# The sum of an attention accumulator's two halves and the gating move from VectorE to GpSimd, with a second ScalarE copy

## The chip, the core and the metric

The kernel runs on one core of a Trainium2 chip. The metric is the device time of one execution in microseconds (us), as the median of several runs; smaller is better.

## What is computed

The reference is a two-layer decoder trunk over 1024 positions of width 1024, all in float32. Each layer normalises its input and projects it; two attention mixers read the projections. The change touches only the end of each mixer: its output is multiplied by its own gate.

```python
# stick-breaking attention, 8 heads of 64
w = where(strict, exp(log_sigmoid(z) + between), 0)      # between: reversed cumulative sum of log_keep
a = einsum('bhqk,bhkd->bqhd', w, v)
a = a.reshape(B, S, SB_WIDTH) * silu(sb_z)
# native sparse attention, 8 heads in 2 groups: compressed, selected and window branches
b = g[0] * o_cmp + g[1] * o_slc + g[2] * o_win
b = b * silu(n_z)
y = sigmoid(m_a) * (a @ w_proj_a) + sigmoid(m_b) * (b @ w_proj_b)
x = x + gate * (y @ w_out)
```

## The kernel before

A layer runs in stages. First come the projections that both mixers need. Then the sparse attention (method `nsa`) and the stick-breaking attention (method `sb`) run one after the other, and in both of them the remaining projections are strewn in on TensorE as filler, by a planner with a fixed cost for each piece. The rest of the filler and the output projections end the layer. In the profiled execution the sparse stage lies from about 316 to 684 us in the first layer and from 1340 to 1735 in the second, the stick-breaking stage from 684 to 945 and from 1735 to 2005.

Every matrix product keeps float32 accuracy by splitting one operand into a high part and a low part, each in the faster float32r format. ScalarE writes the high part (line 136) and VectorE the difference (line 137). The values V lie in memory as 64 columns of high parts beside 64 columns of low parts, so a value product leaves an accumulator `av` of 128 partitions in PSUM: 64 partitions for the high half, 64 for the low half of one head, times 256 query positions. The two halves still have to be added. PSUM holds one such accumulator (`bufs=1`).

The methods that the change touches do this:

- `merge` (line 929 on, stick-breaking stage): ScalarE copies one half to the SBUF tile `mt` (line 935, with a shift of 64 partitions), and VectorE adds the other half to it, reading PSUM, and writes 64 partitions of the output tile `o` (line 936). Two heads share one tile of 128 partitions.
- `finish_pair` (line 921 on): after the odd head of a pair SyncE loads the gate `szl` (line 925), VectorE multiplies (line 926) and SyncE stores to the array AD in HBM (line 927).
- `nsa_merge` (line 1191 on) and `nsa_finish` (line 1199 on) are the same for the sparse stage, with a tile of 64 partitions by 512 columns (two heads side by side), lines 1195, 1196, 1205 to 1207.

One job of the stick-breaking stage is one head and one block m of 256 queries, m = 0 to 3, thus 32 jobs in a layer; a job has two rows of tiles, x = 0 and 1, with 128(2m + x + 1) keys. For each row TensorE computes the scores (lines 885, 886, 888), ScalarE two sigmoids C and E (lines 1298, 1299), VectorE a reversed running product over C (the scan, line 1302) and the product of E with it (line 1303). TensorE transposes E (line 898), ScalarE and VectorE split it into `wh` and `wl` (lines 136, 137), and TensorE multiplies it with the values (lines 917, 918). GpSimd sets one column of C to 1 (line 1294). The scores of a job and the value products of the job before are traced in turn, and `merge` is the last step of the latter.

Each engine works through its queue in order. Who waits for whom is set by semaphores from the data dependencies; the order within a queue is laid out by a scheduler at build time. SyncE's queue holds most DMAs, GpSimd's holds the loads of AD and of a few gates for the output stage (lines 1392, 1458). The tiles `mt` and `szl` have one buffer each.

Of the kernel before, what the change touches and what calls it, by code (L numbers as in the profile page):

```python
# [15 lines left out]
ALU = mybir.AluOpType  # L16
# [71 lines left out]
class Trunk:  # L88
# [832 lines left out]
    def finish_pair(self, pool, o, row, m, gate_row):  # L921

        nc = self.nc
        sz = self.tl(pool, [P, 256], F32, "szl", bufs=1)
        nc.sync.dma_start(sz, self.SZ[gate_row:gate_row + P, m * 256:m * 256 + 256])
        nc.vector.tensor_tensor(o, o, sz, ALU.mult)
        nc.sync.dma_start(self.AD[row:row + P, m * 256:m * 256 + 256], o)

    def merge(self, pool, ps, o, par):

        nc = self.nc
        a = par * 64
        b = 64 - a
        t = self.tl(pool, [P, 256], F32, "mt", bufs=1)
        nc.scalar.copy(t[a:a + 64], ps[b:b + 64, 0:256])
        nc.vector.tensor_tensor(o[a:a + 64], ps[a:a + 64, 0:256], t[a:a + 64], ALU.add)


    def nsa_load_kv(self, g):
# [251 lines left out]
    def nsa_merge(self, pool, ps, o):  # L1191

        nc = self.nc
        t = self.tl(pool, [64, 256], F32, "mt", bufs=1)
        nc.scalar.copy(t, ps[64:128, 0:256])
        nc.vector.tensor_tensor(o, ps[0:64, 0:256].rearrange("p (h t) -> p h t", h=2),
                                t.rearrange("p (h t) -> p h t", h=2), ALU.add)

    def nsa_finish(self, pool, o, hd, m):

        nc = self.nc
        sz = self.tl(pool, [64, 2, 256], F32, "szl", bufs=1)
        c = slice(m * 256, m * 256 + 256)
        r = hd * 64
        nc.sync.dma_start(sz, self.SZ[r:r + P, c].rearrange("(h d) t -> d h t", d=64))
        nc.vector.tensor_tensor(o, o, sz, ALU.mult)
        nc.sync.dma_start(self.AD[512 + r:512 + r + P, c].rearrange("(h d) t -> d h t", d=64), o)

    def av_stages(self, pool, m, es, v):
# [302 lines left out]
```

## Time and profile before

| | |
|---|---|
| median of 3 runs | 2184.01 us (2183.47 to 2190.08) |
| the profiled execution, whole | 2188.37 us |
| its span, which the rows below count | 2186.6 us |
| TensorE busy | 2096.8 us, 96% |
| VectorE busy | 1575.6 us, 72% |
| ScalarE busy | 1130.8 us, 52% |
| GpSimd busy | 72.4 us, 3% |
| DMA | 136 GB/s on average |

The engines are named PE (TensorE), PEld (its weight loads), DVE (VectorE), ACT (ScalarE), POOL (GpSimd) and SP (SyncE) in the profile; a trailing q is an engine's instruction queue. A row names the line of the kernel, the engine, the operation and the tiles, output before input. The ends of matmuls are modelled, and they overlap, so a busy TensorE isn't TensorE at its peak. Who released a wait is inferred from semaphores.

### The profile page before, as it was taken

How to read it: one execution, taken by the hardware profiler on the slowest of the kernel's cores; microseconds unless marked ns; L12 is line 12 of the kernel's file. 1: busy time of each engine (PE TensorE's matmuls, PEld its weight loads, DVE VectorE, ACT ScalarE, POOL GpSimd, SP SyncE). 2: the span in 40 equal slices, each digit the busy share in tenths (PEclk: the TensorE clock that was granted, in tenths of full speed). 3: DMA queues.
4: the chain of work that ended last, by engine and by line, in shares of the span. 5: the costliest groups of instructions: out<-in, count | busy, mean ns of one | idle time of the engine just before them, and what ended most of it. 6: DMA issues, size and time to landing. Idle time of an engine off the chain costs nothing.

```text
span 2186.6 us, 36378 instructions
## 1 busy us (share of the span) xinstructions
PE 2096.8 (96%) x12952; PEld 1817.6 (83%) x12952; DVE 1575.6 (72%) x3698; ACT 1130.8 (52%) x2465; POOL 72.4 (3%) x242
## 2 busy tenths in 40 slices
PE   3999999999999999999999999999999999999999
PEld 3899788988988777779799987889898877777899
DVE  5758568878867778786866763887788687778643
ACT  4433137666666656563533422765666656556410
POOL 2200000000000000010001000000000000001000
PEclk8999999999999999999999999999999999999999
DMA  7445933244226454175456465222532444534433
GB/s 292 96 150 169 287 121 103 87 124 126 80 64 149 126 140 125 64 252 180 157 170 167 137 180 150 84 90 86 145 97 83 121 127 113 145 100 167 154 123 104
DMA packets 254102, 297.02 MB, mean 136 GB/s; under 512 B 38888, under 2 KB 201568, under 8 KB 253920
## 3 DMA queue, kind: packets, MB, share of 16 engines
q1 hardware_dynamic: 213152, 250.65, 38.3%
q10 hardware_dynamic: 36224, 29.37, 5.3%
q0 software_dynamic: 4544, 14.68, 2.4%
q8 instruction: 102, 1.67, 0.3%
q14 instruction: 80, 0.66, 0.1%
HBM read 206.28 MB, written 83.89 MB: 133 GB/s over the span
## 4 chain that ended last, share of the span: by engine, by line
PE 72%; DVE 15%; DMA 4%; issue 4%; ACT 3%; POOL 1%; SPq 0%; DVEq 0%; ACTq 0%; POOLq 0%
PE proj L194 16%; PE proj L198 16%; PE proj L196 16%; PE tr L898 6%; DVE C L1302 5%; PE av L918 4%; PE av L917 3%; PE sc L885 3%; PE sc L886 3%; DVE E L1303 3%; DVE wl L137 2%; DVE w L137 1%; ACT wh L136 1%; DMA ada<-in_ada_w 1%; DMA actlo<-AD 1%
## 5 line engine op out<-in xcount | busy, mean ns | idle before, releaser
L194 PE MATMUL proj<-acthi,w 128*128 128x512 f32 x1312 | 537.5, 410 | 3.4 <-DVE sz L833 2.1
L198 PE MATMUL proj<-acthi,w 128*128 128x512 f32 x1312 | 536.9, 409 | 0.8 <-DVE w L137 0.8
L196 PE MATMUL proj<-actlo,w 128*128 128x512 f32 x1312 | 534.5, 407 | 0.5 <-DVE actlo L137 0.5
L136 ACT CAST w<-raw 128x512 fp32r<-128x512 f32 (+1 forms) x296 | 183.5, 623 | 219.4 <-PE proj L198 111.3
L137 DVE TENSOR_TENSOR wl<-tr,wh 128x512 fp32r<-128x512 f32 (+2 forms) x408 | 255.8, 639 | 46.1 <-ACT wh L136 44.4
L194 PEld LDWEIGHTS proj<-acthi,w 128*128 128x128 f32 x1312 | 249.8, 190 | 40.6 <-DVE sz L833 2.5
L196 PEld LDWEIGHTS proj<-actlo,w 128*128 128x128 f32 x1312 | 249.3, 190 | 37.7 <-DVE actlo L137 1.9
L198 PEld LDWEIGHTS proj<-acthi,w 128*128 128x128 f32 x1312 | 249.0, 190 | 37.5 <-DVE w L137 1.3
L136 ACT CAST wh<-tr 128x512 fp32r<-128x512 f32 (+2 forms) x408 | 219.2, 550 | 87.7 <-PE tr L898 84.7
L137 DVE TENSOR_TENSOR w<-raw,w 128x512 fp32r<-128x512 f32 (+1 forms) x296 | 203.3, 690 | 85.0 <-ACT w L136 83.6
L194 PE MATMUL proj<-w,acthi 128*128 128x256 f32 (+1 forms) x768 | 222.0, 289 | 7.1 <-ACT G L813 3.3
L198 PE MATMUL proj<-w,actlo 128*128 128x256 f32 (+1 forms) x768 | 221.3, 288 | 0.0
L196 PE MATMUL proj<-w,acthi 128*128 128x256 f32 (+1 forms) x768 | 220.5, 287 | 0.0
L898 PE MATMUL tr<-ident,E 128*128 128x128 f32 x1152 | 188.7, 275 | 26.1 <-DVE E L1303 25.5
L918 PE MATMUL av<-wl,V 128*128 128x256 f32 (+1 forms) x776 | 202.1, 287 | 5.5 <-DVE wl L137 5.5
L917 PE MATMUL av<-wh,V 128*128 128x256 f32 (+1 forms) x776 | 202.0, 278 | 0.4 <-ACT E L1146 0.2
L898 PEld LDWEIGHTS tr<-ident,E 128*128 128x128 f32 x1152 | 140.3, 140 | 72.0 <-DVE E L1303 40.6
L1302 DVE TENSOR_TENSOR_SCAN C<-C 128x128 f32<-128x128 f32 (+7 forms) x128 | 173.1, 1352 | 34.3 <-ACT C L1298 33.6
L885 PE MATMUL sc<-kk,q 128*128 128x512 f32 (+3 forms) x512 | 174.2, 340 | 2.1 <-DVE mx L1143 0.9
L886 PE MATMUL sc<-kk,q 128*128 128x512 f32 (+3 forms) x512 | 174.5, 341 | 0.0
L918 PEld LDWEIGHTS av<-wl,V 128*128 128x128 f32 x776 | 146.0, 188 | 25.7 <-DVE wl L137 13.0
L917 PEld LDWEIGHTS av<-wh,V 128*128 128x128 f32 x776 | 146.4, 189 | 13.7 <-ACT wh L136 3.2
(250 smaller groups left out, 3911.1 us busy)
## 6 DMA issues: line engine op xcount, KB each, us to landing
raw<-in_w_in SPq DMA_DIRECT2D x168, 256.0 KB, 3.3
ada<-in_ada_w SPq DMA_DIRECT2D x48, 512.0 KB, 5.5
kk<-QK SPq DMA_DIRECT2D x48, 512.0 KB, 7.7
q<-QK ACTq DMA_DIRECT2D x64, 256.0 KB, 4.6
QK<-s SPq DMA_DIRECT2D x32, 512.0 KB, 3.1
MD<-sz SPq DMA_DIRECT2D x64, 256.0 KB, 2.6
QK<-s SPq DMA_DIRECT2D x48, 256.0 KB, 4.2
VD<-s SPq DMA_DIRECT2D x48, 256.0 KB, 2.1
```

Of the source, the lines that this page charges most:

```text
L136: nc.scalar.copy(hi, src)
L137: nc.vector.tensor_tensor(lo, src, hi.bitcast(F32), ALU.subtract)
L194: nc.tensor.matmul(ps, lh, rh, start=(x == 0), stop=False)
L196: nc.tensor.matmul(ps, lh, rl, start=False, stop=False)
L198: nc.tensor.matmul(ps, ll, rh, start=False, stop=(x == n - 1))
L885: nc.tensor.matmul(ps, q, k[:, 0, c0:c1], start=True, stop=False)
L886: nc.tensor.matmul(ps, q, k[:, 1, c0:c1], start=False, stop=not masks)
L898: nc.tensor.transpose(pt[:, x * P:x * P + P], b, self.ident)
L917: nc.tensor.matmul(ps[:, c:d], lhsT, hi[:, a:b], start=(first and x == 0), stop=False, skip_group_check=True)
L918: nc.tensor.matmul(ps[:, c:d], lhsT, lo[:, a:b], start=False, stop=(last and x == n - 1), skip_group_check=True)
L1302: nc.vector.tensor_tensor_scan(rev, rev, rev, 1.0, ALU.mult, ALU.bypass)
L1303: nc.vector.tensor_tensor(e[:, 0:nk], e[:, 0:nk], c[:, 1:nk + 1], ALU.mult)
```

## The change

In both attention stages ScalarE copies both halves of the accumulator to SBUF, the first to `mt` as before, the second to the output tile `o`. GpSimd adds `mt` to `o` in place, and GpSimd, not VectorE, multiplies the finished tile by the gate. The loads and stores around them stay on SyncE's queue.

```diff
@@ finish_pair
         nc.sync.dma_start(sz, self.SZ[gate_row:gate_row + P, m * 256:m * 256 + 256])
-        nc.vector.tensor_tensor(o, o, sz, ALU.mult)
+        nc.gpsimd.tensor_tensor(o, o, sz, ALU.mult)
         nc.sync.dma_start(self.AD[row:row + P, m * 256:m * 256 + 256], o)
@@ merge
         nc.scalar.copy(t[a:a + 64], ps[b:b + 64, 0:256])
-        nc.vector.tensor_tensor(o[a:a + 64], ps[a:a + 64, 0:256], t[a:a + 64], ALU.add)
+        nc.scalar.copy(o[a:a + 64], ps[a:a + 64, 0:256])
+        nc.gpsimd.tensor_tensor(o[a:a + 64], o[a:a + 64], t[a:a + 64], ALU.add)
@@ nsa_merge
         nc.scalar.copy(t, ps[64:128, 0:256])
-        nc.vector.tensor_tensor(o, ps[0:64, 0:256].rearrange("p (h t) -> p h t", h=2),
-                                t.rearrange("p (h t) -> p h t", h=2), ALU.add)
+        nc.scalar.copy(o, ps[0:64, 0:256].rearrange("p (h t) -> p h t", h=2))
+        nc.gpsimd.tensor_tensor(o, o, t.rearrange("p (h t) -> p h t", h=2), ALU.add)
@@ nsa_finish
         nc.sync.dma_start(sz, self.SZ[r:r + P, c].rearrange("(h d) t -> d h t", d=64))
-        nc.vector.tensor_tensor(o, o, sz, ALU.mult)
+        nc.gpsimd.tensor_tensor(o, o, sz, ALU.mult)
```

## Rows read from the trace of the kernel before

**Rows 1.** Busy time by stage: stretch, its length, PE, PEld, DVE, ACT, POOL.

```profile
316.00:684.00 368.00, 365.78 (x2371) 322.28 (x2370) 290.28 (x880) 238.46 (x563) 1.94 (x13) 1.00 0.36 105
684.00:945.00 261.00, 245.18 (x1404) 198.80 (x1403) 209.69 (x280) 162.09 (x355) 11.60 (x68) 1.00 0.44 122
1340.00:1735.00 395.00, 392.98 (x2494) 343.52 (x2493) 301.60 (x927) 245.92 (x583) 1.41 (x10) 1.00 0.35 102
1735.00:2005.00 270.00, 254.17 (x1449) 205.87 (x1448) 215.06 (x290) 165.31 (x362) 11.77 (x70) 1.00 0.44 121
```

**Rows 2.** Waits of TensorE: us in total, times, longest.

```profile
PE tr L898 <- DVE E L1303: 25.5, 38, 1.1
...
PE av L918 <- DVE wl L137: 5.5, 12, 0.9
```

**Rows 3.** Timeline of VectorE, one head of stick-breaking: start, us, instruction.

```profile
789.57 1.75 DVE L1302 TENSOR_TENSOR_SCAN C<-C 128x768 f32<-128x768 f32 x1
791.45 0.96 DVE L1303 TENSOR_TENSOR E<-E,C 128x768 f32<-128x768 f32 x1
...
799.14 2.28 DVE L1302 TENSOR_TENSOR_SCAN C<-C 128x1024 f32<-128x1024 f32 x1
801.56 1.23 DVE L1303 TENSOR_TENSOR E<-E,C 128x1024 f32<-128x1024 f32 x1
```

**Rows 4.** Timeline of TensorE, the same head, with idle time before.

```profile
792.47 0.55 PE L898 MATMUL tr<-ident,E 128*128 128x128 f32 x3 [0.50 <-DVE E L1303]
...
802.84 0.55 PE L898 MATMUL tr<-ident,E 128*128 128x128 f32 x3 [0.33 <-DVE E L1303]
```

**Rows 5.** Groups by line, VectorE: busy us, mean ns, idle before.

```profile
L936 DVE TENSOR_TENSOR o<-av,mt 64x256 f32<-64x256 f32 x64 | 26.7, 417 | 31.6 <-ACT mt L935 30.8
L1196 DVE TENSOR_TENSOR o<-av,mt 64x256 f32<-64x256 f32 x64 | 26.5, 414 | 27.9 <-ACT mt L1195 27.5
...
L1206 DVE TENSOR_TENSOR o<-o,szl 64x512 f32<-64x512 f32 x32 | 21.8, 682 | 0.3
...
L926 DVE TENSOR_TENSOR o<-o,szl 128x256 f32<-128x256 f32 x32 | 13.5, 423 | 0.8
```

**Rows 6.** The chain that ended last: start, us on it, what.

```profile
323.89 0.04 DVE o L1196
...
850.11 0.38 ACT mt L935
...
857.99 0.44 DVE o L936
...
1995.51 0.33 DVE o L926
```

**Rows 7.** Timeline of ScalarE, the same head, with idle time before.

```profile
784.40 0.60 ACT L1298 ACTIVATE C<-sc 128x512 f32<-128x512 f32 x1 [0.21 <-PE sc L886]
...
789.99 0.37 ACT L935 COPY mt<-av 64x256 f32<-64x256 f32 x1 [0.28 <-PE av L918]
791.48 0.60 ACT L1298 ACTIVATE C<-sc 128x512 f32<-128x512 f32 x1 [1.13 <-PE sc L886]
...
799.98 0.37 ACT L935 COPY mt<-av 64x256 f32<-64x256 f32 x1 [0.73 <-PE av L918]
...
801.96 0.28 ACT L1298 ACTIVATE C<-sc 128x128 f32<-128x128 f32 x1 [1.62 <-PE sc L888]
```

**Rows 8.** Groups by line, GpSimd.

```profile
L745 POOL MEMSET xs<- 128x1056 f32 x4 | 3.9, 986 | 0.0
...
L738 POOL MEMSET VCS<- 128x512 f32 x2 | 1.1, 527 | 93.6 <-PE av L918 93.3 <-POOLq L1505 0.3
```

**Rows 9.** Timeline of GpSimd at the start of the kernel.

```profile
12.63 1.24 POOL L153 TENSOR_TENSOR nr0t<-nr0t,nr0v 128x4 f32<-128x4 f32 x1
...
20.96 0.20 POOL L153 TENSOR_TENSOR nr0t<-nr0t,nr0v 128x4 f32<-128x4 f32 x1
```

**Rows 10.** Timeline of VectorE at the same place, eight operations merged.

```profile
11.21 9.33 DVE L481 SCALAR_TENSOR_TENSOR acc<-ada,silu_c,acc 128x1024 f32<-128x1024 f32 x8
```

## The prediction

> **What bounds the kernel now.** The page's first part, read first, has TensorE as by far the busiest engine and VectorE as the second (the table above), so an edit that takes work from VectorE can pay only where TensorE has a hole that VectorE made. The table by stage, read next, shows where such holes are [rows 1]. In the two stretches of the sparse attention (316 to 684 and 1340 to 1735 us) TensorE is busy 365.8 of 368 and 393.0 of 395 us: 4.2 us of holes together. In the two stretches of the stick-breaking attention (684 to 945 and 1735 to 2005) it is busy 245.2 of 261 and 254.2 of 270 us: 15.8 us of holes each, with VectorE at 80%. The waits of TensorE name the cause: 25.5 us, in 38 waits, were for VectorE's product E (line 1303), and 5.5 us for the low halves wl [rows 2]. So the stick-breaking stage is the place where this change can gain or lose. There a scan on VectorE, then the multiply that makes E, then the transposes on TensorE run one after another: at 789.57 the scan of 768 columns takes 1.75 us, the multiply starts at 791.45, and the transposes that stood waiting start at 792.47 [rows 3, 4]. The same happens with the scan of 1024 columns at 799.14, the multiply at 801.56 and the transposes at 802.84. I looked at this head; there are 16 (8 in each of two layers) of the same shape.
>
> **What the change removes.** VectorE loses 64 + 64 merges at 0.417 and 0.414 us, 32 gates of the sparse stage at 0.682 and 32 of the other at 0.423: 26.7 + 26.5 + 21.8 + 13.5 = 88.5 us [rows 5]. Little of it lies on the path. In the chain that ended last these four lines have 31 pieces, the first at 323.89 us (0.04 us) and the last at 1995.51 (0.33 us); I added them up: 6.9 us [rows 6]. Most merges stand where VectorE would otherwise wait for the next transposes and their ScalarE copy. Where one does stand between a scan and its multiply it costs up to 0.44 us (857.99 us). VectorE also stood 58.3 us idle in front of merges, waiting for ScalarE's first copy [rows 5]; but what follows such a merge mostly needs TensorE too, which in those places is busy with projections. I count the 6.9 us as the whole gain: -6.9.
>
> **What it adds on ScalarE.** 128 copies at 0.37 us, the duration of the first copy, are 47 us more, on an engine at 162 to 165 us of 261 and 270 in the stage that matters [rows 1, 7]. Behind the second copy wait the next sigmoids and the casts wh, on which the scans and the value matmuls depend. In the head that I looked at, the three copies in VectorE's busy stretch have 0.21, 1.13 and 1.62 us of idle time before the sigmoid that follows; the shortest, in front of the sigmoid at 784.40, is the one that doesn't cover 0.37, so that sigmoid comes 0.16 us later [rows 7]. 16 x 0.16 = +2.6 us. In the chain the first copy has five pieces, four of them of 0.38 us as at 850.11 [rows 6]; there the second adds its own 0.37: +1.5 us. The bank of the accumulator comes free after the second copy, not after VectorE's merge, hence earlier; no row shows TensorE waiting for that bank, so I count nothing.
>
> **What it adds on GpSimd.** 128 adds and 64 gates on an engine that did almost nothing in these stages (1.4 to 11.8 us each [rows 1]). Its rows of before show only small two-input operations and write-only memsets. The price of an add of 256 columns I bound so. Memsets of 512 and 1056 columns took 527 and 986 ns: 0.84 ns for each further column [rows 8]. One pass over 256 columns is then 0.22 us, the lower end. Three passes one after the other (two reads, one write) are 0.65, and with the whole of the 0.20 us that a four-column operation takes [rows 9] it is 0.85, the upper end. No row is nearer to one end, so I take the middle, 0.53.
>
> By the Trainium skill (GPSIMD Engine Reference, section 3.1) a two-input add of 2048 columns takes 4497 ns, by which 256 columns would be an estimated 0.56 us; with it the sum below would come out 1 us higher.
>
> **Where the adds meet VectorE.** One place of the trace shows both engines reading SBUF at once. While VectorE ran eight scalar-tensor-tensor operations from 11.21 us on [rows 10], a GpSimd operation of four columns took 1.24 us; at 20.96, with VectorE idle, the same line took 0.20 [rows 9]. GpSimd got through only when VectorE's operation was over. No row shows VectorE waiting for GpSimd, since those operations are too short to hold anything up. I forecast that it holds in both directions. Now place the add. In the head shown, the first copy starts at 789.99; with the second the add is ready at about 790.73, in the middle of the scan (789.57 + 1.75 = 791.32). It waits until 791.32 and then runs, 0.13 us before the multiply would start (791.45): the multiply comes 0.53 - 0.13 = 0.40 us later, and the transposes, which stand waiting for it, too. The copy at 799.98 puts its add at 800.72, inside the scan that ends at 801.42: again 0.40 [rows 3, 7]. The third add of the stretch finds no scan or multiply behind it, and the gates follow when the multiply is done. So two hits in each of 16 heads: 32 x 0.40 = +12.8 us; at the lower price 32 x 0.09 = 2.9, at the upper 32 x 0.72 = 23.
>
> The Trainium skill (SBUF — State Buffer, section Who interferes with whom) speaks against the change in the same sense: a VectorE instruction with two SBUF inputs and a GpSimd instruction that reads SBUF share one port pair, and whichever comes second is blocked entirely. The trace agrees for GpSimd as the second (1.24 against 0.20 us); for VectorE as the second no run here shows it yet.
>
> **Waits that move.** The add waits for the second copy, the gate for the load szl. Behind them in GpSimd's queue stand the one-column memsets of C, the memset of the selection stage and, at each layer's end, loads for the output. The memsets run as soon as their buffer comes free, ahead of the scans that use it. SyncE's store of the gated output now waits for GpSimd, later by one or two operations; behind it on that queue stand the reload of szl, weight loads and stores of projections. The weights are loaded a group ahead of use, so I count nothing; if that cover is gone, a late load costs up to 2 us at each layer's end. ScalarE's first copy now waits for GpSimd to have read mt, whose single buffer was used at least a microsecond earlier. In the sparse stage TensorE's projections cover everything: 0, with ends of -4.2 (all its holes) and +6 (64 adds at 0.09).
>
> **The sum.** -6.9 + 2.6 + 1.5 + 12.8 = +10.0 us; by the ends of the add's price +0.1 and +20. The profiled execution took 2188.37 us, 1.8 of them outside its span, and is 4.4 above the median of the runs, 2184.01. On the profiled one it gives 2198, on the median 2194.
>
> **Rivals.** First: GpSimd takes its turn without holding VectorE up, or the multiply goes ahead of it. For it: no row shows VectorE delayed. Then only -6.9 + 4.1 = -2.8 stays: 2181. Second, on the other side: VectorE, free of 88 us and of its stands in front of the merges, starts scans earlier, since the scheduler lays out its queue anew. It decides from the point where the 31 us that TensorE waits for E and wl [rows 2] fall by 4, which with the -2.8 makes 6.8; if a third of them goes, -10.3 - 2.8 gives 2171. Against it: the waits come after a scan that itself started without a hole (1.75 us scan, multiply 0.13 later). Third: GpSimd's queue itself becomes late, gates and stores with it, and output loads or memsets hold up TensorE at the ends of the layers or the heads: 2 x 4 us on top of the forecast, 2202. For it: the loads for the output share that queue; against it: TensorE has projections left there.
>
> **How the numbers follow.** Some 0.3% (6.6 us) is what a measurement can tell from no change. The forecast gets 0.47, of which 0.38 is slower by more than that and 0.09, the lower prices, within it; the first rival 0.25 (0.22 within, 0.03 faster); the second 0.18, faster; the third 0.10, slower. Faster 0.21, within 0.31, slower 0.48. The range leaves out the outer part of the second rival and the worst of the third: 2174 to 2208; the forecast's own is 2184 to 2204.
>
> **What would show it.** The merge on GpSimd should take 0.3 to 0.9 us beside an idle VectorE and up to 2 us longer behind a scan. The multiplies of 768 and 1024 columns should begin, or end, some 0.4 us later after their scans, and TensorE's waits for E should grow from 25.5 to about 38 us. If they don't grow, the first rival holds; if they shrink, the second. The sparse stretches should keep their length to a few us. Were the sparse stage to grow by 10 us, or the schedule of TensorE to be laid out differently, the prediction is wrong in its basis.

## The result and the profile after

The changed kernel takes 2207.61 us (median; 2205.65 to 2209.07) against 2183.74 of the kernel before beside it: the ratio is 1.0101, with a 95% interval of 1.008 to 1.0122. It is slower, by some 22 to 24 us, where the forecast was +10. The page of after, first its span, then busy time, share of the span and instructions of each engine:

```profile
span 2206.1 us, 36565 instructions
...
PE 2097.4 (95%) x12952; PEld 1817.0 (82%) x12952; DVE 1522.3 (69%) x3506; ACT 1171.4 (53%) x2593; POOL 257.8 (12%) x434
```

The split of work came out as the change says: GpSimd now has 12% of the span, VectorE 69%. To see where the time went I cut both profiles at the same events and not at the same times: a sparse stretch begins with its first matmul of line 1040 and ends with its last first copy (line 1195), a stick-breaking stretch ends with its last first copy (line 935), the stretch "output, 1" runs from there to the first product of line 1436, "output and layer 2" on to the sparse stretch of layer 2, "output, 2" to the end (line numbers of before). Lengths in us, worked out from the traces:

| stretch | before | after | difference |
|---|---|---|---|
| up to the first sparse stretch | 296.8 | 290.5 | -6.3 |
| sparse, layers 1 and 2 | 379.6, 372.7 | 383.9, 377.5 | +9.1 |
| stick-breaking, layers 1 and 2 | 266.7, 266.8 | 267.8, 267.7 | +2.0 |
| output, 1 | 51.5 | 60.5 | +9.0 |
| output and layer 2, up to its sparse stretch | 367.3 | 367.6 | +0.3 |
| output, 2 | 185.2 | 190.6 | +5.4 |

The first line holds none of the changed work. Its length is 288 to 292 us in most profiles below and 296 to 298 in three, before's among them (in before TensorE is busy for 253.8 us of it at a mean granted clock of 0.94 of full speed, in after for 248.8 at 0.96), so that line is left out of the reading. Each length is read from one profiled execution. In the kernels below that leave a stage alone, the two sparse stretches together are 750.9 to 752.9 us, the two stick-breaking ones 533.3 to 534.9, "output, 1" 51.5 to 54.3: differences of that size mean nothing. The other lines say it: most of the loss is in the output and in the sparse stage, and the stick-breaking stage, on which the forecast rested, grew by 2 us, hardly more than that scatter. The windows of after by the same cuts are below, with the columns of [rows 1] (stretch, length, PE, PEld, DVE, ACT, POOL, then TensorE's clock, DMA share, GB/s):

```profile
290.50:674.40 383.90, 378.54 (x2431) 332.34 (x2430) 284.06 (x875) 250.77 (x607) 45.64 (x54) 0.99 0.34 99
674.40:942.20 267.80, 250.88 (x1434) 203.32 (x1433) 199.77 (x237) 175.37 (x393) 54.30 (x115) 1.00 0.44 120
942.20:1002.70 60.50, 52.76 (x238) 42.13 (x236) 37.78 (x61) 29.74 (x53) 9.22 (x13) 0.94 0.63 206
1370.20:1747.70 377.50, 371.51 (x2399) 326.06 (x2398) 282.98 (x872) 250.61 (x606) 44.69 (x53) 1.00 0.35 101
1747.70:2015.40 267.70, 251.15 (x1435) 203.26 (x1434) 199.52 (x237) 175.38 (x393) 54.05 (x115) 1.00 0.44 120
2015.40:2206.10 190.70, 181.47 (x1150) 162.63 (x1148) 93.36 (x166) 50.20 (x85) 9.51 (x13) 0.99 0.42 135
```

In the sparse stretches TensorE has holes of 5.4 and 6.0 us (length less busy time), where by the same cuts before had 2.4 and 2.0; in the third row it is busy 52.8 of 60.5 us, at a mean granted clock of 0.94. What it waited for (whole run: us in total, times, longest):

```profile
PE tr L898 <- DVE E L1304: 30.9, 38, 1.5
...
PE proj L194 <- DVE gt L1463: 11.6, 5, 5.5
...
PE sc L885 <- DVE mx L1135: 3.4, 4, 1.5
...
PE tr L1079 <- DVE cpg L1068: 1.5, 2, 0.8
```

The waits for E grew by 5.4 us from [rows 2], not by the 12 to 13 of the forecast. New is the wait for `gt`, the first products of the output. And the sparse stage shows waits for VectorE's maxima and products. GpSimd's own lines (busy us, mean ns | idle before):

```profile
L937 POOL TENSOR_TENSOR o<-o,mt 64x256 f32<-64x256 f32 x64 | 64.6, 1009 | 117.8 <-ACT o L936 116.4 <-POOL C L1295 0.3
L1198 POOL TENSOR_TENSOR o<-o,mt 64x256 f32<-64x256 f32 x64 | 49.9, 780 | 693.6 <-ACT o L1197 613.8 <-DVE E L1167 79.9
L1207 POOL TENSOR_TENSOR o<-o,szl 64x512 f32<-64x512 f32 x32 | 41.7, 1303 | 2.5
L926 POOL TENSOR_TENSOR o<-o,szl 128x256 f32<-128x256 f32 x32 | 30.4, 951 | 3.2 <-DMA szl<-SZ 0.9
```

An add that VectorE did in 0.42 us [rows 5] takes 0.78 us in the sparse stage and 1.01 in the other; the shortest of both kinds takes 0.72.

### The profile page after: what moved, and what is told of

Same layout as the page of the kernel before. It is cut to its first block, busy times and chain, and to the rows that moved or that the text cites. A ratio compares the mean times of both kernels' runs of the same rounds, so it can differ in the third digit from the quotient of the medians.

```text
span 2206.1 us, 36565 instructions
## 1 busy us (share of the span) xinstructions
PE 2097.4 (95%) x12952; PEld 1817.0 (82%) x12952; DVE 1522.3 (69%) x3506; ACT 1171.4 (53%) x2593; POOL 257.8 (12%) x434
## 4 chain that ended last, share of the span: by engine, by line
PE 70%; DVE 15%; DMA 6%; ACT 4%; issue 2%; POOL 1%; SPq 0%; DVEq 0%; ACTq 0%; POOLq 0%
PE proj L194 16%; PE proj L198 16%; PE proj L196 16%; PE tr L898 6%; DVE C L1303 4%; PE av L918 3%; PE av L917 3%; PE sc L885 3%; PE sc L886 3%; DVE E L1304 3%; DVE wl L137 2%; DVE w L137 1%; DMA gt<-MD 1%; ACT wh L136 1%; PE tr L436 1%
## 5 line engine op out<-in xcount | busy, mean ns | idle before, releaser
L198 PEld LDWEIGHTS proj<-acthi,w 128*128 128x128 f32 x1312 | 248.8, 190 | 36.4
```

Of the source, the lines that this page charges most:

```text
L198: nc.tensor.matmul(ps, ll, rh, start=False, stop=(x == n - 1))
```

## The experiments

All ratios are against the kernel before, run beside it on the same chip.

**One stage at a time.** The first kernel has only the hunks of the change in `nsa_merge` and `nsa_finish`, the second only those in `merge` and `finish_pair`:

```diff
# nsa_only, nsa_merge and nsa_finish alone
+        nc.scalar.copy(o, ps[0:64, 0:256].rearrange("p (h t) -> p h t", h=2))
+        nc.gpsimd.tensor_tensor(o, o, t.rearrange("p (h t) -> p h t", h=2), ALU.add)
...
+        nc.gpsimd.tensor_tensor(o, o, sz, ALU.mult)
# sb_only, merge and finish_pair alone
+        nc.scalar.copy(o[a:a + 64], ps[a:a + 64, 0:256])
+        nc.gpsimd.tensor_tensor(o[a:a + 64], o[a:a + 64], t[a:a + 64], ALU.add)
...
+        nc.gpsimd.tensor_tensor(o, o, sz, ALU.mult)
```

> Only the sparse stage is changed (copy, add and gate there as in the changed kernel), the stick-breaking stage is as before. Theory A (three separate prices: the output's gate loads stand behind the last merge in GpSimd's queue, about 13 us for two layers; the sparse stage has grown by 4.2 and 4.8 us; the stick-breaking stage by 1.1 and 0.9): +9 us, with the output stages as before. Theory B (my prediction: the price is VectorE held up in the stick-breaking stage, the sparse stage costs nothing): within 3 us of the kernel before.

Measured: 2192.43 us, ratio 1.0044 [1.0028, 1.0059]. The sparse stretches are 384.3 and 377.8 us, the others within 2 us of before.

> Only the stick-breaking stage is changed. Theory A: +2 us in the stage and +13 us where the output starts, thus +15 in all, with TensorE's wait for the first gt product of 5 to 6 us in each layer. Theory B: most of the +24 us of the whole change, spread over the 16 heads.

Measured: 2197.58 us, ratio 1.007 [1.0053, 1.0087]. The stick-breaking stretches are 267.5 us each, the output stretches 59.9 and 191.3, with 12.3 us of waits for `gt`. The sparse stretches, which this kernel leaves alone, are 378.3 and 372.6: the measure for the others. The two effects add up to about the whole, and each belongs to its stage.

**The start of the output.** In after, the first four loads `gt` of the output stand on GpSimd's queue behind its last merge and gate. GpSimd in after (start, us, instruction, idle before), then ScalarE's sigmoid on that load and TensorE's matmuls before and after the wait:

```profile
942.65 2.41 POOL L937 TENSOR_TENSOR o<-o,mt 64x256 f32<-64x256 f32 x1 [7.02 <-ACT o L936]
945.14 0.74 POOL L926 TENSOR_TENSOR o<-o,szl 128x256 f32<-128x256 f32 x1
945.82 2.20 POOL L1459 DMA_DIRECT2D gt<-MD  x4
...
951.21 0.63 ACT L1461 ACTIVATE gt<-gt 128x512 f32<-128x512 f32 x1 [8.05 <-DMA gt<-MD]
...
946.71 0.40 PE L198 MATMUL proj<-acthi,w 128*128 128x512 f32 x1
952.62 0.80 PE L194 MATMUL proj<-acthi,w 128*128 128x512 f32 x1 [5.51 <-DVE gt L1463]
```

GpSimd stood idle for 7.02 us, waiting for the second copy of the last merge, with the loads behind it. In before they had gone out seven us ahead of the last merge, which was on VectorE, since no part of it stood on that queue (GpSimd, then VectorE):

```profile
936.62 2.15 POOL L1458 DMA_DIRECT2D gt<-MD  x4 [5.49 <-ACT w L136]
...
943.62 0.43 DVE L936 TENSOR_TENSOR o<-av,mt 64x256 f32<-64x256 f32 x1
```

The merge itself takes 2.41 us here. Beside it VectorE runs two-input splits of line 137 back to back, up to 944.46, and the merge ends 0.60 us after them. TensorE pays twice for its wait of 5.51 us: the granted clock stood at its lower level, 1.2 GHz (0.50 of full speed), from 949.8 to 956.6, so the first matmul after the wait takes 0.80 us where the last one before it took 0.40. TensorE's busy time in this stretch is 52.8 us against 50.1 in before, so some 2.7 of the 9.0 us are not wait but matmuls that run slower. In layer 2 it waited 5.1 us, and the clock stood at that level for 3.4 us. To test the cause of the wait, the last job of a layer alone (head 7, block 3), 2 of 128 merges, goes back to VectorE:

```diff
+        if last:
+            nc.vector.tensor_tensor(o[a:a + 64], ps[a:a + 64, 0:256], t[a:a + 64], ALU.add)
+            return
...
-        nc.gpsimd.tensor_tensor(o, o, sz, ALU.mult)
+        eng.tensor_tensor(o, o, sz, ALU.mult)
...
+                    last = head == 7 and m == 3
+                                         nc.vector if last else nc.gpsimd)
```

> The changed kernel, but the merge and the gate of the very last stick-breaking job of each layer (head 7, block 3) stay on VectorE as before: 2 of 128 merges. Theory A: the first four gate loads go out some 9 us earlier, TensorE's waits of 5.5 and 5.1 us for the first gt product are gone, and 11 to 14 us come back: +10 to +13 against the kernel before. Theory B (contention): 2 of 128 merges are worth 0.4 us, so +23 stays.

Measured: 2193.04 us, ratio 1.0046 [1.0031, 1.0061]; 14.6 us less than after by the medians, 12 by the ratios. TensorE's instructions stand in the very order of after. GpSimd issues the loads here at

```profile
935.16 2.21 POOL L1464 DMA_DIRECT2D gt<-MD  x4
```

and the waits for `gt` fall from 11.6 to 1.6 us; the output stretches are 51.3 and 185.4 us, as before. This is over half of the loss, and its cause is shown: two sums and their gates in front of the loads.

With the same cure and the sparse stage as before, only the stick-breaking stage is left:

> Only the stick-breaking stage is changed, except its last job in each layer, whose sum and gate stay on VectorE. Theory: of the 13.5 us that this stage's change costs, 12 to 14 are the late loads for the output behind GpSimd's last operations, and the hold on VectorE's multiplies is worth 1 us in each layer: the whole at -1 to +3 us against before, the stick-breaking stretches at 267.5 us, TensorE's waits for E near 31 us. Rival: the hold matters more than the stretches show; then +5 us or more stays.

Measured: 2183.9 us, ratio 1.0002 [0.999, 1.0013], stick-breaking stretches of 267.5 and 267.4 us, 31.0 us of waits for E. So with 62 of the 64 merges of that stage on GpSimd the change costs nothing there that can be measured.

**The copies without GpSimd.** Both copies on ScalarE, adds and gates on VectorE:

```diff
-        nc.gpsimd.tensor_tensor(o[a:a + 64], o[a:a + 64], t[a:a + 64], ALU.add)
+        nc.vector.tensor_tensor(o[a:a + 64], o[a:a + 64], t[a:a + 64], ALU.add)
# and so for the other add and the two gates
```

> Both copies on ScalarE as in the changed kernel, but the adds and the gates on VectorE, from SBUF; GpSimd does nothing new. Theory A: the second copy is nearly free, so the output start and the 9 us of the sparse stage are back: within 4 us of the kernel before. Rival C (the second copy on ScalarE, or the new order of the queues that it brings, is what costs in the sparse stage): +8 or more, with the sparse stretches 4 us longer each as in the changed kernel.

Measured: 2188.37 us, ratio 1.0025 [1.0015, 1.0035], a little over the 4 us expected. The attention stretches are 378.1 and 373.1, and 265.9 and 265.9 us: the second copy costs nothing there, and in the stick-breaking stage 0.8 and 0.9 us are won. The loss is again in the output (56.8 us, where kernels that leave it alone have 51.5 to 54.3): VectorE, in order, stands before a gate whose load lands late,

```profile
945.01 0.43 DVE L926 TENSOR_TENSOR o<-o,szl 128x256 f32<-128x256 f32 x1 [2.61 <-DMA szl<-SZ]
```

and the first products `gt` stand behind it. I took that wait for the cause of the 4.3 us and gave `szl` a second buffer, so that each load goes out a job earlier:

```diff
-        sz = self.tl(pool, [P, 256], F32, "szl", bufs=1)
+        sz = self.tl(pool, [P, 256], F32, "szl", bufs=2)
```

> Both copies on ScalarE in both stages, sums and gates on VectorE as in the run without GpSimd, and in the stick-breaking stage two buffers for the gate's load szl instead of one, so that each load is issued a job earlier. Theory: what that run lost (4.3 us) was the last load of szl in each layer, which landed 8.9 us after its issue and held up VectorE and with it the first products gt; then the y stage falls from 56.8 to about 52 us and the whole to 2181 to 2184 us, at or a little under the kernel before, since the four attention stretches were 0.5 us shorter or equal. Rival: the loss lies in the order of projections, copies and casts around the output; then it stays at 2187 to 2189.

Measured: 2187.95 us, ratio 1.0016 [1.0004, 1.0027]: a miss. The gate no longer waits (it runs at 938.33 with no idle time before), but the output stretch is still 56.0 us. ScalarE in this kernel:

```profile
943.01 0.62 ACT L136 CAST yh<-gt 128x512 fp32r<-128x512 f32 x1 [3.44 <-DVE gt L1468]
943.54 0.62 ACT L136 CAST w<-raw 128x512 fp32r<-128x512 f32 x1
946.58 0.63 ACT L1461 ACTIVATE gt<-gt 128x512 f32<-128x512 f32 x1 [2.43 <-DMA gt<-MD]
```

Here the cast `yh` stands ahead of a weight cast and waits 3.44 us for the product; in before the weight cast at 949.47 went ahead of `yh` at 950.00. So the order of work around the output, laid out anew, fits what this trace shows; that it accounts for the whole loss of this kernel was not tried.

**The sparse stage.** It has hardly a hole on TensorE, and VectorE and GpSimd run beside each other in it. Three kernels change that stage alone and put something else on GpSimd. The first puts memsets of nearly the same duration (0.72 and 1.17 us, where sums and gates take 0.73 and 1.28) in the place of sums and gates, so that GpSimd writes and doesn't read; in this branch the halves are not summed and the outputs not gated. The second writes one column; the third makes every sum twice:

```diff
# nsa_write_only (mt and szl are the first columns of wider tiles)
-        nc.gpsimd.tensor_tensor(o, o, t.rearrange("p (h t) -> p h t", h=2), ALU.add)
+        nc.gpsimd.memset(big, 0.0)      # 64x750
-        nc.gpsimd.tensor_tensor(o, o, sz, ALU.mult)
+        nc.gpsimd.memset(big, 0.0)      # 64x1290
# nsa_tiny
+        nc.gpsimd.memset(t[:, 0:1], 0.0)
+        nc.gpsimd.memset(sz[:, 0, 0:1], 0.0)
# nsa_double
+        nc.gpsimd.tensor_tensor(sp, o, t.rearrange("p (h t) -> p h t", h=2), ALU.add)
```

> As the run with only the sparse stage changed, but GpSimd's adds and gates there are memsets that write a scratch part of the same tiles for about as long (0.7 and 1.2 us) and read nothing; so the output of the sparse branch lacks the sum of the halves and the gate. TensorE's order is that of the run with only the sparse stage changed in all but 20 of 13104 places. Theory A1 (GpSimd's reads hold up VectorE's instructions with two SBUF inputs): the 4.7 and 5.1 us of the two sparse stretches vanish, the kernel is within 2 us of the one before. Rival A2 (the new order of TensorE's work costs them): both stretches stay at 384 and 378 us, +9.

> Only the sparse stage is changed, and there GpSimd does not do the sums and gates: in their place it writes one column (the halves are not summed and the outputs not gated in this branch, so the output is not the reference's). ScalarE's two copies, the queue that each step stands in and TensorE's order are those of the kernel with the sparse stage changed (13084 of 13104 places). Theory 'beside': the sparse stretches grow because GpSimd's operations run, for 0.73 and 1.28 us each, beside VectorE's; with next to no running time they fall from 384.3 and 377.8 to 378.5 and 373 us, and the whole to within 2 us of before. Theory 'order': it is the order of work, laid out anew, that costs; then the stretches stay near the 382.6 and 374.8 of the run with plain memsets, and the whole near +6 us.

> Only the sparse stage is changed, and there every sum on GpSimd is made twice (the second into a spare tile): 64 more operations of about 0.73 us. Theory 'beside': the 88 us in which GpSimd now runs in these stretches cost some 10 us; 47 us more cost some 5 more: stretches of about 387 and 380 us, the whole at +12 to +15. Theory 'order': no change against the kernel with the sparse stage changed, 384 and 378, the whole at +8.4 within 2.

| kernel | on GpSimd | sparse stretches, us | median, us | ratio |
|---|---|---|---|---|
| nsa_tiny | one column written | 377.5, 374.6 | 2183.82 | 0.9995 [0.9984, 1.0007] |
| nsa_write_only | memsets nearly as long as the sums and gates | 382.6, 374.8 | 2190.02 | 1.0031 [1.0019, 1.0043] |
| nsa_only | sums and gates | 384.3, 377.8 | 2192.43 | 1.0044 [1.0028, 1.0059] |
| nsa_double | sums twice, and gates | 384.1, 380.7 | 2197.22 | 1.0054 [1.0035, 1.0072] |

With next to nothing on GpSimd, and the copies, queues and TensorE's order kept, the loss is gone: 752.1 us for both stretches against 750.9 in the kernel that leaves the stage alone. With the sums and gates it is 762.1, so up to 10 us of the loss come from what GpSimd runs there. Of these an estimated 1.7 are TensorE's clock: near the start of the first sparse stretch, before the first sum, it stood at its lower level, 1.2 GHz, for 6.8 us in `nsa_only`, as in before, but for 3.4 in `nsa_tiny`. The doubled sums add 2.7 us there (in an execution that took 8 us more than their median, most of it in the first line of the table by stretches), where 5 were expected, and the intervals of the two ratios overlap: a price for each sum is not shown. The memsets missed their expectation, which was to be within 2 us of before; they sit between. Which of VectorE's operations pay tells why. Groups by line and tile, 128x256 and 128x128 columns, in the first sparse stretch (busy us, mean ns), first after, then the kernel with one column, then the one with memsets:

```profile
L1167 DVE TENSOR_SCALAR E<-E,f 128x256 f32<-128x256 f32 x8 | 3.9, 508 | 0.1
...
L1072 DVE TENSOR_TENSOR cpg<-cs,cgr 128x128 f32<-128x128 f32 x2 | 1.6, 775 | 0.1
```

```profile
L1166 DVE TENSOR_SCALAR E<-E,f 128x256 f32<-128x256 f32 x8 | 2.6, 350 | 0.1
...
L1071 DVE TENSOR_TENSOR cpg<-cs,cgr 128x128 f32<-128x128 f32 x2 | 0.6, 292 | 0.1
```

```profile
L1166 DVE TENSOR_SCALAR E<-E,f 128x256 f32<-128x256 f32 x8 | 4.5, 582 | 0.1
...
L1071 DVE TENSOR_TENSOR cpg<-cs,cgr 128x128 f32<-128x128 f32 x2 | 0.6, 292 | 0.1
```

The product of two SBUF tiles (`cpg`) is slowed by GpSimd's sums and gates and not by its memsets; the scaling of E, one input, by both. Beside the memsets 39 of VectorE's operations with two SBUF inputs ran, and none took over 0.01 us longer than its shape takes in the kernel with one column. The Trainium skill says this in SBUF — State Buffer, section Who interferes with whom: "A DVE instruction with two SBUF inputs contends with a GpSimd instruction that reads SBUF, not with one that only writes it", while it counts a tensor_scalar among the operations that can take both port pairs; the trace agrees in both halves (775 against 292 ns; 508 and 582 against 350). One such hit, in after, on VectorE and on GpSimd:

```profile
503.64 1.26 DVE L1072 TENSOR_TENSOR cpg<-cs,cgr 128x128 f32<-128x128 f32 x1
...
503.45 1.29 POOL L1207 TENSOR_TENSOR o<-o,szl 64x512 f32<-64x512 f32 x1
```

The gate began 0.19 us earlier and ends at 504.74; the product, 0.29 us by itself, ends at 504.90. It stood still until the gate was over. Against the same shapes in the kernel with one column, VectorE's operations that ran beside GpSimd's and took over 0.05 us longer add up to 6.0 us of such delay in the first sparse stretch of after and 6.1 in the second (12 operations each), with the memsets to 5.8 and 3.2, nearly all of it in the scaling.

One rival is not excluded by a run of its own. With one column on GpSimd, SyncE no longer waits for GpSimd before its stores (5.9 us in all, against 182.5 for the gates in `nsa_only`, up to 14.7 at a time). But TensorE's waits in the sparse stretches of `nsa_only` name VectorE, but for one of 0.5 us for a load.

A fourth kernel brings the gates of this stage back to VectorE (its gate line is that of before):

> Only the sparse stage is changed, and there only the copies and the adds (0.73 us each); the gates (1.3 us each) are VectorE's again. Theory A1: the delays of VectorE behind gates go (in the changed kernel they are 8 of the 15 slowed instructions of the first stretch, about 5 of 6.6 us), so about two thirds of the 9 us come back: +3. Rival A2 (order): +9 stays, or an unrelated size.

Measured: 2194.71 us, ratio 1.0055 [1.0038, 1.0072], stretches of 384.1 and 377.2 us: nothing came back, a miss. The delays of VectorE beside GpSimd did fall, from 5.9 us in each stretch of `nsa_only` to 3.2 and 3.0. VectorE's wait list has what may have taken their place:

```profile
DVE o L1206 <- POOL o L1197: 30.6, 20, 4.3
DVE o L1206 <- POOL C L1294: 7.0, 2, 3.5
```

The gate on VectorE waits, in order, for GpSimd, 37.6 us in all (30.6 of them named for a sum) and up to 4.3 at a time, and what stands behind it waits too. That this made up for the delays saved is argued, not shown.

**The hold in the stick-breaking stage.** The forecast had two hits of 0.40 us in each head. In the head of [rows 3, 7], as it runs in after, VectorE, then GpSimd, then GpSimd's group of these memsets in the whole run:

```profile
788.29 1.75 DVE L1303 TENSOR_TENSOR_SCAN C<-C 128x768 f32<-128x768 f32 x1
790.18 1.22 DVE L1304 TENSOR_TENSOR E<-E,C 128x768 f32<-128x768 f32 x1
...
800.54 1.23 DVE L1304 TENSOR_TENSOR E<-E,C 128x1024 f32<-128x1024 f32 x1
...
802.29 0.97 DVE L1303 TENSOR_TENSOR_SCAN C<-C 128x128 f32<-128x128 f32 x1
```

```profile
789.66 0.92 POOL L937 TENSOR_TENSOR o<-o,mt 64x256 f32<-64x256 f32 x1 [1.06 <-ACT o L936]
...
801.83 0.10 POOL L1295 MEMSET C<- 128x1 f32 x1 [4.47 <-ACT w L136]
802.01 0.97 POOL L937 TENSOR_TENSOR o<-o,mt 64x256 f32<-64x256 f32 x1
```

```profile
L1295 POOL MEMSET C<- 128x1 f32 x128 | 12.2, 97 | 301.4 <-DVE E L1304 243.4 <-ACT E L1300 36.3 <-ACT C L1299 11.4
```

The first hit is there: the multiply starts 0.14 us after its scan, as before, but takes 1.22 us instead of 0.96, for the add ends only at 790.58. It is so in all 16 heads (1.20 to 1.22 us in after, 0.94 to 0.96 in before). The second hit is there in 4 of the 16 (1.48 to 1.76 us instead of 1.23), but not in this head: the add was ready at 799.76, when the second copy ended, but ahead of it on GpSimd's queue stood the one-column memset of C, which can run only when a multiply has freed its buffer, here that of 1024 columns, which ends at 801.77 (the row names ScalarE's cast, which ended 0.07 us later; over all these memsets the multiply E is named for 243.4 of 301.4 us of idle time, last row). So the add came at 802.01, behind that multiply (1.23 us, as before), and held up a scan of 128 columns (0.97 us instead of 0.42), for which TensorE shows no wait. To test that, the memset of C goes to VectorE, in after and, as a control, in before:

```diff
-                nc.gpsimd.memset(hs["c", x][:, nk:nk + 1], 1.0)
+                nc.vector.memset(hs["c", x][:, nk:nk + 1], 1.0)
```

> The changed kernel, but the one-column memset of C goes to VectorE. In the changed kernel the add of block 3 was ready about 0.6 us before the scan of 1024 columns ended, but stood behind a memset in GpSimd's queue that waited for the multiply to end, so it missed that multiply. Theory: without the memset in front the add hits the multiply of 1024 columns as I had forecast for it, and TensorE's waits for E grow from 30.9 to 35 or more us; against its control (the kernel before with the same memset on VectorE) the waits for E grow by 9 or more. Rival (the missed hit has another reason): the waits for E stay near 31.

> Control for the run with the column memset on VectorE: the kernel before with the same memset on VectorE, 128 small instructions more there. Expected within 5 us of the kernel before, with waits for E of 25 to 28 us.

Measured: 2212.9 us, 1.0134 [1.0119, 1.0149] for after with the memset moved; 2183.87, 1.0006 [0.9997, 1.0016] for the control. In the first, the stick-breaking stretches are 269.6 and 269.8 us, 2 more than in after, the waits for E 33.2 us in 46, and the missing hit is there (GpSimd, then VectorE, at the same place):

```profile
801.29 1.03 POOL L937 TENSOR_TENSOR o<-o,mt 64x256 f32<-64x256 f32 x1 [7.92 <-ACT o L936]
...
801.90 1.50 DVE L1304 TENSOR_TENSOR E<-E,C 128x1024 f32<-128x1024 f32 x1
```

1.50 instead of 1.23 us; in 14 of the 16 heads this multiply now takes 1.32 to 1.79. In the control the stretches are 266.5 and 266.9 and the waits 23.9, a little under the 25 to 28 expected: moving the memset costs nothing by itself. The waits for E grew less than the 35 us that were expected, but against the control by 9.3, as expected. So the memset in front of the add is shown to be what kept the hit away.

## Why the forecast was too small

**The direction was right** and came in part for the reason that the forecast named, GpSimd holding VectorE up. But two terms that it put at nothing, the sparse stage and the output, came to some 9 and 14 us, and the large term was too big. That the measured 2207.6 us still lies inside the stated range, at its very end (2208), is luck in the main: the forecast's own span ended at 2204, and 2208 was drawn for the second rival and the third. Term by term:

| step of the forecast | forecast, us | measured, us | from |
|---|---|---|---|
| merges leave the path | -6.9 | no gain in the sparse stage; not tried alone in the other | 752.1 us of sparse stretches with one column on GpSimd, 751.2 with both copies and the sums on VectorE |
| second copies enter it | +4.1 | nothing in either attention stage | both copies without GpSimd: -1.7 stick-breaking, -1.1 sparse |
| hold in the stick-breaking stage | +12.8 | some +4 (+2.0 against before) | 535.5 us of stretches against 531.8 without GpSimd, and 533.5 before |
| sparse stage | 0 (-4.2 to +6) | +8 to +10 | 762.1 against 752.1 us, of which 1.7 clock; +9.1 in after |
| output loads behind GpSimd's work | 0 (third rival: 2 x 4) | +14 (12 to 14.6) | the last job back on VectorE |

*The hold.* Its mechanism was right, in both directions: the add waits for the scan's end, and the multiply for the add's. The step that failed first is its size, "the multiply comes 0.53 - 0.13 = 0.40 us later". It came 0.26 us later: the add ends 0.54 us after the scan, and the multiply, 0.96 us by itself, 0.82 us after the add, so 0.14 of it passed while it was held. That the 0.54 is nearly the 0.53 of the forecast is luck: the add takes 0.72 us by itself, 0.19 more than priced, and 0.18 of it pass while it waits for the scan. And the step "two hits in each of 16 heads" failed at the queue: the prediction listed the memsets of C that stand in GpSimd's queue and said that they run ahead of the scans; it didn't ask whether one of them would hold the add back. It did, until the multiply was over, and so 20 of the 32 hits came, worth 5.7 us on the multiplies instead of 12.8. The waits for E grew by 5.4 us, those for E and wl together by 2.2.

*The sparse stage.* The step "TensorE's projections cover everything" failed. In before TensorE was busy for all but 4.2 us [rows 1], which I took as proof of cover. A stage without holes has cover only as long as its VectorE chain keeps pace: small products of the compressed branch and the scaling of E, which matmuls wait for, were now delayed by up to 1.0 and 0.6 us, and TensorE also waited longer for the maxima (up to 1.5 us, before up to 0.5), which stand in the same queue. The range of that term ended at 64 x 0.09 = 6, a hold priced from the other stage's geometry; in fact a 64x512 gate of 1.29 us made a product of 0.29 us take 1.26. The contention was used in one stage and forgotten in the other. The prediction had named its own sign of being wrong in its basis, a sparse stage longer by 10 us, and it came within 1 us of that (+9.1).

*The output.* This was the third rival, named with its cause, priced at 2 x 4 us and given 0.10. That price had no row behind it, and the sum took it as nothing because "TensorE has projections left there"; they ran out, and TensorE waited 5.5 and 5.1 us for the first `gt`. The trace of before could have given such a row: the loads had gone out at 936.62, and the last merge, which waits for its accumulator, ran at 943.62. Put behind a merge that ends at 945.06 and its gate, they go out 9.2 us later in after. The prediction says that loads for the output stand behind the adds in GpSimd's queue; the step that was missing is to look up when each is issued and when the instruction put in front of it will have its inputs.

The second rival, a gain from a schedule laid out anew, didn't come: TensorE waited 33.2 us for E and wl, before 31.0. The first, no hold, is excluded by the 1.20 to 1.22 us of all 16 multiplies of 768 columns.

## What to carry to other kernels

An engine that is 3% busy may still hold a queue that matters: before work goes onto it, list every DMA on that queue with its issue time, and compare that with the time at which the new work's last input is ready. An engine's short operations beside VectorE are priced by what they fall on: look in every stage, also in those without a hole, for VectorE operations with two SBUF inputs that feed a matmul at once. And a merge that waits for the end of a chain belongs on the engine whose queue has nothing behind it: two merges of 128, put back with their gates, returned over half of the loss.

## What the runs showed of the hardware beyond the forecast

- GpSimd's add of 64x256 columns takes 0.72 us by itself (502.65 us in after, line 1198), its gate of 64x512 1.28, VectorE's 0.42 and 0.68 [rows 5]. The Trainium skill (GPSIMD Engine Reference, section 3.1) gives 4497 ns for an add of 2048 columns, by which 256 would be an estimated 0.56 us; the trace has 0.16 more.
- The hold goes both ways: a 0.29 us product stood until a 1.29 us gate had ended, and a 0.72 us add took 2.41 us beside a row of VectorE's two-input splits. A scan holds an add to its end: 26 adds of after that began 0.18 to 1.46 us before the end of a scan all ended 0.51 to 0.54 us after it.
- What is held loses a little less than it waits: 0.18 us of a 0.72 us add and 0.14 of a 0.96 us multiply passed during the wait.
- The record of a VectorE instruction that is held up shows the wait as its own duration, not as idle time before it (1.22 instead of 0.96 us at 790.18); a comparison of equal tile shapes gives it away.
